# A strided attention kernel whose store of groups 20 and 21 is issued in three parts

## The chip, the cores and the metric

The kernel runs on one core of a Trainium2 chip. The metric is device time in microseconds (us): 127.87 us is the median of three runs (127.7 to 128.3). A core has a matrix engine (PE, TensorE), a vector engine (DVE), a scalar engine (ACT), a general engine (POOL, GpSimd), and SyncE (SP), which here only issues transfers. Sixteen transfer engines move data between the chip's large memory (DRAM) and the on-chip memory of 128 partitions. An instruction that issues a transfer only hands it over; the transfer then waits in a queue and adds to a semaphore when it has landed.

## The reference

```
for i in range(seq):                       # seq = 1024
    attend_positions = np.arange(0, seq, stride)          # stride = 64: 16 positions
    q = Q[:, :, i:i+1, :]; k = K[:, :, attend_positions, :]; v = V[:, :, attend_positions, :]
    scores  = np.einsum('bhqd,bhkd->bhqk', q, k) / np.sqrt(dim)
    weights = np.exp(scores - np.max(scores, axis=-1, keepdims=True))
    weights = weights / (np.sum(weights, axis=-1, keepdims=True) + 1e-10)
    result[:, :, i, :] = np.einsum('bhqk,bhkd->bhqd', weights, v)[:, :, 0, :]
```

Q, K, V and the result are 8 x 12 x 1024 x 64 in float32. Each of the 96 heads reads all its 1024 query rows, but only 16 key and 16 value rows. So Q (25.2 MB) is read once, the result (25.2 MB) is written once, and the keys and values count for little.

## The kernel before

The 96 heads are worked on in 24 groups of four heads (1 MB of Q and 1 MB of result each). `big` is an on-chip ring of 16 group buffers, 8 KB per partition each. A group's Q is loaded into its buffer (`load`), cast to bf16 half by ACT and half by POOL (`cast_a`, `cast_p`), turned by DVE (`turn`), multiplied with the keys on PE (`scores`), brought back by DVE (`spread`), and made into weights by DVE, POOL and ACT (`maximum`, `subtract`, `raise_`, `add_up`, `invert`, `normalise`). PE multiplies the weights with the values (`outputs`), and ACT copies the products over the group's Q in the same buffer (`evict`, two halves `a` and `b`). From there the group is stored.

All transfers are issued by SP, on one queue, in an order written out by hand (`order`, worked off by `issue`): all early loads; then for groups 0 to 9 a store of one group, followed for groups 2 to 9 by the load that reuses an older buffer; then stores of two groups at a time, 10 to 21; and at the very end, behind a barrier of all engines, the store of 22 and 23 (`end = send(NG - 2, 2)`). The store of 20 and 21 is thus the last but one. `send` (line 250) makes one transfer of 128 rows: a row is one partition of `big`, for two groups 16 KB in one piece on chip and four pieces of 4 KB in DRAM.

A list of operations (`Program.op`) records for each what it reads, writes and on which semaphore ("lane") it counts. Lanes whose name begins with `out` are stores; POOL waits for all of them (lines 620 to 623), clears the semaphores, and this goes on while the last store is under way, which it does not wait for. SP itself waits for the last store (line 655), and then the kernel ends. A tile `edge` (128 x 32) is declared and not used.

Of the kernel before, what the change touches and what calls it, by code (L numbers as in the profile page):

```python
# [18 lines left out]
def _ap_with(ap: bass.AP, new_ap, extra_offset: int = 0) -> bass.AP:  # L19
    return dataclasses.replace(  # L20
        ap, ap=[list(p) for p in new_ap], offset=ap.offset + extra_offset
    )


def _copy(nc, out: bass.AP, in_: bass.AP):

    sides = [
        mybir.BassSymbolicTensorAccessPattern(
            ap=side.ap, dtype=side.dtype, bass_ap=side,
            is_dma=True, for_custom_bir_dma=True,  # L30
        )
        for side in (in_, out)
    ]
    return nc.sync.add_instruction(  # L34
        mybir.InstDMACopy(
            name=nc.get_next_instruction_name(), engine=mybir.EngineType.SP,
            ins=sides[:1], outs=sides[1:], queue="qSPDynamicHW",
            mode="Copy",
        )
    )  # L40


class Program:
# [13 lines left out]
    def op(self, engine, fn, reads=(), writes=(), after=(), lane=None, gate=None, gates=(), looped=False, late=False, last=False):  # L57
        i = len(self.ops)
        deps, own = set(after), set()
        for k in reads:  # L60
            deps.add(self.writer.get(k))
            own.add(self.writer.get(k))
        for k in writes:
            deps.update(self.readers.get(k, ()))
            deps.add(self.writer.get(k))
            own.add(self.writer.get(k))
        deps.discard(None)
        for k in reads:
            self.readers.setdefault(k, []).append(i)
        for k in writes:  # L70
            self.writer[k], self.readers[k] = i, []
        self.ops.append(dict(
            engine=engine, fn=fn, lane=lane or engine, deps=deps, own=own,
            gate=gate, gates=gates, last=last, late=late, looped=looped or engine == "PE",
        ))
        return i
# [96 lines left out]
def kernel(  # L173
# [8 lines left out]
    nc = tc.nc  # L182

    B, H, S, D = Q.shape
# [3 lines left out]
    P = 128  # L188
    HG = 4
# [3 lines left out]
    SD = S * D  # L193
    NB = 16
    TURN = 2
    FIRST, LAST, ROUNDS = 2, 22, 4
    AHEAD = 3
    EPS = 1e-10
    assert NH == NG * HG == 96 and S == 1024 and D == 64 and NK == 16

# [3 lines left out]
    edge = sb.tile([P, 32], FP32, name="edge")  # L204
# [4 lines left out]
    big = sb.tile([P, NB, 32 * D], FP32, name="big")  # L209
# [25 lines left out]
    op = prog.op  # L235
# [7 lines left out]

    def store(g, n):
        b = g % NB
        op("SP", lambda: send(g, n), lane=f"out{b}",
           reads=[f"b{i % NB}{h}" for i in range(g, g + n) for h in "ab"])

    def send(g, n):
        o = big[:, g % NB : g % NB + n]  # L250
        return _copy(
            nc,
            _ap_with(out, [[16 * D, P], [2 * SD, 2 * n], [1, 16 * D]], g * HG * SD),
            _ap_with(o, [o.ap[0], [1, 1], [1, 32 * n * D]]),
        )

# [14 lines left out]
    def constants():  # L271
# [11 lines left out]
        for i in range(2):  # L283
            op("DVE", lambda i=i: nc.vector.memset(ex[i], EPS), writes=[f"ex{i}"])
        op("DVE", lambda: nc.vector.memset(k_cur, 0.0), writes=["k_cur0", "k_cur1"])
# [22 lines left out]
    def value_sums(n):  # L308
        for c in range(2):
            r = nc.tensor.matmul(  # L310
                o_ps[n][:, c, 0 : NC * D // 2],
                lhsT=perm_v[:, n].rearrange("p b e u k -> p (b e u k)"),
                rhs=v_bf[:, 6 * c : 6 * c + 6], start=True, stop=True,
            )
        return r
# [46 lines left out]
    def place_k(g):  # L362
        n = 1 if g < 2 else 2
        gap = k_cur[:, 0, 0, 32:].bitcast(I32)
        op("POOL", lambda: nc.gpsimd.tensor_copy(  # L365
            out=_ap_with(gap, [gap.ap[0], [80, 2 * n], [32, 2], [1, 16]], 160 * (g % 2)),
            in_=k_all[:, g : g + n].rearrange("p g f b x -> p (g f) b x").bitcast(I32),
        ), reads=["k_zero"] + [f"k{i % 2}{s}" for i in range(g, g + n) for s in range(4)],
           writes=[f"k_cur{i % 2}" for i in range(g, g + n)], gate=None if g == 1 else "stK")
# [9 lines left out]
    def scores(g):  # L379
        op("PE", None, reads=[f"qt{g % 2}", f"k_cur{g % 2}"], writes=[f"sc{g % 2}"],  # L380
           gates=[("turned", g + 1)] + [("stK", g // 2 + 1)] * (g % 2 == 0), gate="sc")
# [93 lines left out]
    def issue(done, flush=False):  # L475
        while order:
            kind, g, some = order[0]
            need = g + some - 1 if kind == "S" else g - NB + 1
            if not flush and need > done:
                return  # L480
            order.pop(0)
            if kind == "L":
                load(g)
            else:
                store(g, some)

    def on(f, g, *a, **how):
        if 0 <= g < NG:
            f(g, *a, **how)

    def next_keys(g):
        if g < NG:
            place_k(g)
        elif g < NG + AHEAD:
            op("POOL", lambda: nc.gpsimd.nop(), gate="stK")

    for n in range(NG + 4):
# [16 lines left out]
        if n == NG - 1:  # L514
            for g in range(AHEAD):
                op("DVE", lambda: nc.vector.nop(), gate="turned", late=True)
# [11 lines left out]
        on(normalise, n - 1)  # L528
        if n + 1 < NG + AHEAD:
            scores(n + 1)  # L530
# [14 lines left out]
    def pe_stream(sems, gates):  # L545
        pe = nc.tensor

        def score_products(g):
            for e in range(2):
                for f in range(2):  # L550
                    r = pe.matmul(  # L551
                        sc_ps[g % 2], lhsT=k_cur[:, g % 2, f, 32 * (1 - e) : 32 * (1 - e) + P],
                        rhs=_ap_with(
                            qt[g % 2], [qt[g % 2].ap[0], [D, 8], [16 * D, 2], [2, 32]],
                            extra_offset=8 * D * e + f,
                        ),
                        start=e + f == 0, stop=e + f == 2,
                    )
            r.then_inc(gates["sc"], 1)
# [14 lines left out]
        for n in range(2):  # L574
            value_sums(n).then_inc(sems["PE"], 1)
        for g in range(AHEAD):
            pe.wait_ge(gates["turned"], g + 1)
# [3 lines left out]
        with pe.Fori(0, NG // TURN):  # L581
            for j in range(TURN):
                pe.wait_ge(gates["turned"], j + AHEAD + 1)
                if j:
                    pe.wait_ge(gates["stK"], (j + AHEAD) // 2 + 1)
                score_products(j + AHEAD)
# [33 lines left out]
    with tc.tile_critical(sync_engine=mybir.EngineType.Pool, no_gpsimd_drain=True) as landed:  # L620
        for sem, n in pending:
            nc.gpsimd.wait_ge(sem, n)
        nc.clear_and_free_semaphores(sems)
    tc.no_sync_barrier()
    end = send(NG - 2, 2)
    tc.declare_no_dep(end.ins, landed, reason="waits for the older stores alone")
# [33 lines left out]
```

## Time and profile before

| | |
|---|---|
| median of three runs | 127.87 us (127.7 to 128.3) |
| profiled execution | 127.99 us |
| its span in the trace | 126.2 us |
| busy: DVE, ACT, POOL, PE | 75%, 72%, 67%, 47% of the span |
| moved by the transfer engines | 51.15 MB, mean 405 GB/s |
| stores of two groups | 7, of 2048 KB each, median 16.9 us from issue to landing |

Times in the trace count from the start of the span; the profiled execution is 1.8 us longer than its span. Views used below: the page with its busy shares and its 40 slices; the waits of SP's queue; the chain of work that ended last, in order of time; the timelines of SP and POOL; groups of instructions by source line; and a table of busy time by stage, whose last two columns are the mean busy share of the sixteen transfer engines and the GB/s that they moved. Transfers issued on SP's queue are marked SPq. A transfer packet counts in the stage in which it starts.

### The profile page before, as it was taken

The numbers are of one execution on the slowest core, as the hardware profiler recorded it, in microseconds if no ns is written. First come the engines' busy times: TensorE is split into PE (matmuls) and PEld (weight loads), VectorE is DVE, ScalarE is ACT, GpSimd is POOL, SyncE is SP. The second block draws the span as 40 slices with busy tenths as digits, with TensorE's granted clock in tenths as the row PEclk, the third lists the DMA queues.
The fourth block names the chain that finished last, engine by engine and source line by source line (L and its number), as shares of the span: only waits on it lengthen the run. The fifth ranks groups of instructions, "written<-read, shape, count | busy, mean of one in ns | idle before, by whom it ended". The sixth has DMA issues, their size and how long they took to land.

```text
span 126.2 us, 1652 instructions
## 1 busy us (share of the span) xinstructions
PE 59.9 (47%) x496; PEld 29.0 (23%) x496; DVE 94.9 (75%) x160; ACT 90.6 (72%) x106; POOL 84.2 (67%) x108
## 2 busy tenths in 40 slices
PE   0002822539766456645666456645666369700000
PEld 0001100114333223333333223333333135300000
DVE  5349699399999999999999999999998985000000
ACT  4043977635999899998999899998997597910000
POOL 3018550929899899999999899998999586000000
PEclk9999995555899999999999999999999999996555
DMA  3999989999899989989999989989999999999990
GB/s 65 355 398 428 467 363 478 405 447 467 363 478 405 447 361 426 493 356 428 465 392 436 470 374 462 462 358 493 389 421 426 428 415 431 431 431 421 426 415 31
DMA packets 6803, 51.15 MB, mean 405 GB/s; under 512 B 3760, under 2 KB 3760, under 8 KB 3760
## 3 DMA queue, kind: packets, MB, share of 16 engines
q1 hardware_dynamic: 6800, 51.12, 97.3%
q14 instruction: 3, 0.02, 0.0%
HBM read 25.95 MB, written 25.17 MB: 405 GB/s over the span
## 4 chain that ended last, share of the span: by engine, by line
DVE 61%; PE 9%; DMA 6%; issue 3%; ACT 2%; POOL 2%; SPq 1%; ACTq 1%; DVEq 1%
DVE qt L356 21%; DVE s_t L384 11%; DVE top L391 11%; DVE total L409 10%; PE sc L551 7%; DMA big<-in_V_dram 6%; DVE w_t L431 5%; DVE rec L416 3%; PE o L565 2%; POOL s_t L398 1%; DVE v_all L334 1%; ACT big L447 1%; SPq L34 1%; ACT qb L347 1%; ACTq L161 1%
## 5 line engine op out<-in xcount | busy, mean ns | idle before, releaser
L447 ACT COPY big<-o 128x1024 f32<-128x1024 f32 x48 | 46.2, 1014 | 1.6 <-PE o L565 1.6
L551 PE MATMUL sc<-qt,k_cur 128*128 128x512 bf16 x108 | 32.3, 424 | 27.4 <-DVE qt L356 22.1
L398 POOL TENSOR_TENSOR s_t<-s_t,top 128x512 f32<-128x512 f32 x24 | 25.4, 1059 | 10.2 <-DVE top L391 10.2
L565 PE MATMUL o<-v_cur,w_t 64*64 64x256 bf16 x384 | 26.5, 277 | 10.3 <-DVE w_t L431 7.7
L356 DVE STREAM_TRANSPOSE qt<-qb 128x1024 int32<-128x1024 int32 x24 | 28.9, 1203 | 0.0
L423 POOL TENSOR_TENSOR w_n<-ex,rec 128x512 bf16<-128x512 f32 x24 | 25.5, 1063 | 2.8 <-DVE rec L416 1.1
L352 POOL CAST qb<-big 128x1024 bf16<-128x1024 f32 x24 | 25.1, 1045 | 0.7 <-DMA big<-in_Q_dram 0.7
L347 ACT CAST qb<-big 128x1024 bf16<-128x1024 f32 x24 | 25.3, 1055 | 0.3 <-DMA big<-in_Q_dram 0.3
L565 PEld LDWEIGHTS o<-v_cur,w_t 64*64 64x64 bf16 x384 | 19.9, 108 | 22.8 <-ACT big L447 16.1
L404 ACT ACTIVATE ex<-s_t 128x512 f32<-128x512 f32 x24 | 15.2, 632 | 9.5 <-POOL s_t L398 9.0
L384 DVE STREAM_TRANSPOSE s_t<-sc 128x512 f32<-128x512 f32 x24 | 16.3, 678 | 3.9 <-PE sc L551 2.6
L551 PEld LDWEIGHTS sc<-qt,k_cur 128*128 128x128 bf16 x108 | 8.7, 101 | 45.1 <-DVE qt L356 30.2
L409 DVE TENSOR_REDUCE total<-ex 128x32 f32<-128x544 f32 x24 | 17.0, 707 | 0.6 <-ACT ex L404 0.6
L391 DVE TENSOR_REDUCE top<-s_t 128x32 f32<-128x512 f32 x24 | 15.5, 648 | 0.1
L431 DVE STREAM_TRANSPOSE w_t<-w_n 128x256 int32<-128x256 int32 x24 | 10.4, 435 | 1.2 <-POOL w_n L423 1.2
L416 DVE RECIPROCAL rec<-total 128x32 f32<-128x32 f32 x24 | 7.5, 312 | 0.0
L310 PE MATMUL o<-big,perm_v 128*128 128x384 bf16 x4 | 1.5, 521 | 12.0 <-POOL big L318 12.0
L373 POOL COPY v_cur<-v_all 128x256 int32<-128x256 int32 (+1 forms) x13 | 5.0, 386 | 0.5 <-PE o L565 0.5
L365 POOL COPY k_cur<-k_all 128x128 int32<-128x128 int32 (+1 forms) x13 | 3.7, 283 | 2.1 <-ACT k_all L303 1.8
L293 ACT CAST big<-big 128x384 bf16<-128x384 f32 x1 | 0.5, 511 | 5.1 <-DMA big<-in_K_dram 5.1
L294 POOL CAST big<-big 128x384 bf16<-128x384 f32 x1 | 0.5, 509 | 5.0 <-DMA big<-in_K_dram 5.0
L303 DVE COPY k_all<-big 32x384 bf16<-32x384 bf16 x6 | 3.5, 591 | 0.1
(19 smaller groups left out, 16.2 us busy)
## 6 DMA issues: line engine op xcount, KB each, us to landing
big<-in_Q_dram SPq DMA_DIRECT2D x24, 1024.0 KB, 12.3
out_dram<-big SPq DMA_DIRECT2D x7, 2048.0 KB, 16.9
out_dram<-big SPq DMA_DIRECT2D x10, 1024.0 KB, 14.2
big<-in_K_dram SPq DMA_DIRECT2D x1, 384.0 KB, 5.8
big<-in_V_dram SPq DMA_DIRECT2D x1, 384.0 KB, 8.2
```

Source lines behind the costliest of these rows:

```text
L347: op("ACT", lambda: nc.scalar.copy(b[:, half:], q[:, half:]), reads=[f"b{g % NB}{h}" for h in "ab"], writes=[f"qb{g % 4}1"])
L352: op("POOL", lambda: nc.gpsimd.tensor_copy(out=b[:, 0:half], in_=q[:, 0:half]), reads=[f"b{g % NB}{h}" for h in "ab"] + [f"qb{g % 4}1"] * ...
L356: return nc.vector.transpose(qt[g % 2].bitcast(I32), qb[g % 4].bitcast(I32))
L384: return nc.vector.transpose(s_t[g % 2].rearrange("p n k -> p (n k)"), sc_ps[g % 2])
L391: return nc.vector.tensor_reduce(out=top[g % 2], in_=s_t[g % 2], op=ALU.max, axis=mybir.AxisListType.X)
L398: op("POOL", lambda: nc.gpsimd.tensor_tensor(out=s_t[g % 2], in0=s_t[g % 2], in1=top[g % 2].unsqueeze(2).to_broadcast([P, 32, NK]), op=ALU ...
L409: return nc.vector.tensor_reduce(out=total[g % 2], in_=ex[g % 2], op=ALU.add, axis=mybir.AxisListType.X)
L423: op("POOL", lambda: nc.gpsimd.tensor_tensor(out=_ap_with(w_n[g % 2], [w_n[g % 2].ap[0], [64, 8], [1, 2], [32, 2], [2, NK]]), in0=ex[g % 2 ...
L431: return nc.vector.transpose(w_t[g % 2].rearrange("p t m -> p (t m)").bitcast(I32), w_n[g % 2].rearrange("p n k -> p (n k)").bitcast(I32),)
L447: op("ACT", lambda: nc.scalar.copy(to, o), reads=[f"o{h}"], writes=[f"b{g % NB}{'ab'[h]}"], gate=None if g == NG - 1 or (g, h) == (NG - 3, ...
L551: r = pe.matmul(sc_ps[g % 2], lhsT=k_cur[:, g % 2, f, 32 * (1 - e) : 32 * (1 - e) + P], rhs=_ap_with(qt[g % 2], [qt[g % 2].ap[0], [D, 8], ...
L565: r = pe.matmul(o_ps[h][rows, t // 2, 256 * (t % 2) : 256 * (t % 2) + 256], lhsT=w_t[g % 2][rows, 4 * h + t], rhs=v_cur[rows, g % 2].rearr ...
```

## The change

The store of groups 20 and 21 becomes three transfers with the same 128 rows in all: rows 0 to 111 on SP's queue; rows 126 and 127 on SP's queue, as a transfer of their own; and rows 112 to 125 on POOL's queue. In front of the last, POOL issues a load of four rows of 64 bytes from Q into the tile `edge`, which nothing reads. Each of the new transfers has its own semaphore, and its name begins with `out`, so POOL also waits for these before it clears the semaphores. All other stores, the last one too, stay at 128 rows.

```diff
+    SPLIT = 20
...
     def store(g, n):
         b = g % NB
-        op("SP", lambda: send(g, n), lane=f"out{b}",
-           reads=[f"b{i % NB}{h}" for i in range(g, g + n) for h in "ab"])
-
-    def send(g, n):
-        o = big[:, g % NB : g % NB + n]
+        rows = [f"b{i % NB}{h}" for i in range(g, g + n) for h in "ab"]
+        if g != SPLIT:
+            op("SP", lambda: send(g, n), lane=f"out{b}", reads=rows)
+            return
+        op("SP", lambda: send(g, n, 0, 112), lane=f"out{b}", reads=rows)
+        op("SP", lambda: send(g, n, 126, 2), lane="out_two", reads=rows)
+        op("POOL", lambda: nc.gpsimd.dma_start(
+            edge[0:4, 0:16], _ap_with(Q, [[D, 4], [1, 16]]),
+        ), lane="out_edge", writes=["edge"])
+        op("POOL", lambda: nc.gpsimd.dma_start(*parts(g, n, 112, 14)), lane="out_some", reads=rows)
+
+    def parts(g, n, p, rows):
+        o = big[p : p + rows, g % NB : g % NB + n]
+        return (
+            _ap_with(out, [[16 * D, rows], [2 * SD, 2 * n], [1, 16 * D]], g * HG * SD + 16 * D * p),
+            _ap_with(o, [o.ap[0], [16 * D, 2 * n], [1, 16 * D]]),
+        )
+
+    def send(g, n, p=0, rows=P):
+        o = big[p : p + rows, g % NB : g % NB + n]
         return _copy(
             nc,
-            _ap_with(out, [[16 * D, P], [2 * SD, 2 * n], [1, 16 * D]], g * HG * SD),
+            _ap_with(out, [[16 * D, rows], [2 * SD, 2 * n], [1, 16 * D]], g * HG * SD + 16 * D * p),
             _ap_with(o, [o.ap[0], [1, 1], [1, 32 * n * D]]),
         )
```

On SP, from the last load to the end of the recorded program, before (-) and with the change (+); `at_ACT` is the count of ACT's finished copies, and x5 means five such rows in a row:

```order
 L34 DMA out_dram<-big 128x2x1024 [waits at_ACT]
 L34 DMA big<-in_Q_dram 128x2048 [waits at_out7]
-L34 DMA out_dram<-big 128x4x1024 [waits at_ACT] x6
-L263 UNCONDITIONAL_BRANCH [waits at_ACT]
+L34 DMA out_dram<-big 128x4x1024 [waits at_ACT] x5
+L34 DMA out_dram<-big 112x4x1024 [waits at_ACT]
+L34 DMA out_dram<-big 2x4x1024
+L279 UNCONDITIONAL_BRANCH [waits at_ACT]
```

The sixth two-group store has become two transfers that stand in its place; the last store (not in the piece) still comes behind the barrier.

On POOL, from the last normalisations to the barrier, with the change (`w_n` are the normalised weights; before, the same rows stand there without the two rows that begin with DMA):

```order
L439 TENSOR_TENSOR w_n_77<-ex_75,rec_85 128x8x2x32 [waits at_DVE]
L389 COPY v_cur<-v_all 128x256 [waits at_PE]
L439 TENSOR_TENSOR w_n_78<-ex_76,rec_86 128x8x2x32 [waits at_DVE]
L253 DMA edge<-in_Q_dram 4x16
L256 DMA out_dram<-big 14x4x1024 [waits at_ACT]
L279 UNCONDITIONAL_BRANCH
L161 UNCONDITIONAL_BRANCH
L161 NO_OP [waits SP_49]
```

The two issues stand behind POOL's last arithmetic and ahead of the barrier; the second waits for ACT's copy of group 21, as SP's store does.

## The prediction

> **What bounds the kernel now.** I read the page first: the busy shares, the 40 slices, and the queues.
>
> ```profile
> PE 59.9 (47%) x496; PEld 29.0 (23%) x496; DVE 94.9 (75%) x160; ACT 90.6 (72%) x106; POOL 84.2 (67%) x108
> ...
> DMA  3999989999899989989999989989999999999990
> GB/s 65 355 398 428 467 363 478 405 447 467 363 478 405 447 361 426 493 356 428 465 392 436 470 374 462 462 358 493 389 421 426 428 415 431 431 431 421 426 415 31
> ...
> q1 hardware_dynamic: 6800, 51.12, 97.3%
> q14 instruction: 3, 0.02, 0.0%
> ...
> DVE 61%; PE 9%; DMA 6%; issue 3%; ACT 2%; POOL 2%; SPq 1%; ACTq 1%; DVEq 1%
> ```
>
> No compute engine is above 75%, but the transfer engines are busy in nearly every slice, and all of it is on one queue, SP's (q1). The chain on the page (last line) names DVE for 61% and the transfers for 6%, but it leads back from the last computation, so I looked at what the end itself waits for: the waits of SP's queue, the last pieces of the chain in order of time, and SP's and GpSimd's timelines near the end.
>
> ```profile
> SPq L655 <- DMA out_dram<-big: 13.7, 1, 13.7
> ...
> 109.01 1.01 ACT big L447
> 110.02 0.91 ACTq L161
> ...
> 106.71 4.93 SPq L34 DMA_DIRECT2D out_dram<-big  x2
> ...
> 105.58 1.06 POOL L423 TENSOR_TENSOR w_n<-ex,rec 128x512 bf16<-128x512 f32 x1
> ```
>
> The last eviction is over at about 110.9 us. SP issues the store of groups 20 and 21 at 106.71 and that of 22 and 23 at about 111.1 (the two together take until 106.71 + 4.93 = 111.64, and one issue takes 0.54). Then SP waits 13.7 us for the last store alone. So the last 14 us of the kernel are transfers already in the queue. GpSimd has nothing after 105.58 + 1.06 = 106.64. A table by stage of those 14 us is the view on which all the rest stands (columns: busy times of the engines with counts, then TensorE's clock, the share of the 16 transfer engines, GB/s):
>
> ```profile
> 118.00:122.90 4.90, 0.00 (x0) 0.00 (x0) 0.00 (x0) 0.00 (x0) 0.00 (x0) 0.50 1.01 428
> 122.90:123.60 0.70, 0.00 (x0) 0.00 (x0) 0.00 (x0) 0.00 (x0) 0.00 (x0) 0.50 0.28 117
> 123.60:124.25 0.65, 0.00 (x0) 0.00 (x0) 0.00 (x0) 0.00 (x0) 0.00 (x0) 0.50 0.06 25
> 124.25:124.90 0.65, 0.00 (x0) 0.00 (x0) 0.00 (x0) 0.00 (x0) 0.00 (x0) 0.50 0.06 25
> 124.90:126.20 1.30, 0.00 (x0) 0.00 (x0) 0.00 (x0) 0.00 (x0) 0.00 (x0) 0.50 0.00 0
> ```
>
> At 428 GB/s each of 16 engines moves 26.75 GB/s, so one row of a two-group store (16,384 bytes) takes 0.61 us on its engine. The view counts a row where it starts: 117 GB/s x 0.70 us is 82 KB, five rows; 25 GB/s x 0.65 us is 16 KB, one row, and again one row in the next window. A share of 0.06 is one engine of 16. So the engines do not finish together: most are through by about 123.6, some four run on to about 124.2, and one single engine is still moving rows until about 125. A 128-row store gives each engine eight rows (128/16). **The end is set by one engine that is about one row behind the next and two to three behind most.** The trace names no engine, so which of the sixteen it is stays unknown.
>
> **The change part by part.** (a) The store of 20 and 21 on SP shrinks from 128 to 112 rows, 112/16 = seven per engine: 0.61 us less on every engine's queue. (b) Two rows go on SP's queue as a store of their own: +0.61 us on two engines. (c) Fourteen rows go on GpSimd's queue: +0.61 us on fourteen engines, if each takes one. The sum over the engines is 112 + 2 + 14 = 128 rows, as before; no byte is saved. If (b) and (c) fell on sixteen different engines, nothing would change; if they overlap on two, two engines have nine rows and two have seven. The time of the end is that of the late engine, so it goes by its own count: seven rows, -0.61; eight, 0; nine, +0.61. These are the bounds of this term. Two of sixteen engines could be the ones with seven, so I take eight, 0.
>
> (d) When they run matters less than how many there are. GpSimd's rows are issued from about 107 on, beside SP's queue, which then still holds nearly three stores (20 and 21, issued at 106.7, land 4.9 us before the last, at about 120.5: 13.8 us of work). A row served early pushes the engine's own rows back by 0.61, and the seven-row share gives that back. The end of an engine that has eight rows in all stays.
>
> (e) Issues on SP: one more, the 2-row one. The 23 loads and 17 stores issued so far cost (ns, least, median, most), and the third line has the stores' time from issue to landing:
>
> ```profile
> L34 SPq DMA_DIRECT2D big<-in_Q_dram x23: 471/594/3505, 1.9 to 77.9; - x23
> L34 SPq DMA_DIRECT2D out_dram<-big x17: 538/615/750, 33.3 to 111.1; - x17
> ...
> DMA to landing us min/median/max: 9.3/14.3/21.2
> ```
>
> One issue is 0.54 to 0.75 us. It lies between 107.3 and 108.0, and SP waits there anyway for the eviction that ends at 110.9: nothing.
>
> (f) Issues on GpSimd: two, a kind the trace of before does not show on that engine. Nearest rows: 0.59 us (the median above) to 3.5 us (the longest issue on SP), so 1.2 to 7.0 us for both; none cheaper than 0. I take 1.2, the common case of the nearest row. From 106.64 they end at 107.8, or at 113.6. Behind them on GpSimd stand only the barrier that SP's last store passes, the wait for the older stores, and the clearing of semaphores. The last store is now issued at 111.1 and so could be up to 2.5 us late. It has cover: its 2 MB take 4.9 us at 428 GB/s and have landed at about 111.1 + 14.3 = 125.4, so the first engines start on it only at about 118. Cost 0 up to some 11 us of issue time; beyond that each microsecond counts in full. GpSimd's later waits on three more stores lie before SP's own wait: the older stores have landed about 4.9 us before the last. 0.
>
> (g) The load of four short rows and the extra completions: at most a few small packets on an engine. Bounds: 0 to one row time, 0.61, since even a full row would not cost more; I take 0.02. (h) GpSimd's rows may move in four pieces of 4 KB each. The slowest full slice above ran at 355 GB/s, the last stage at 428: a row would take 0.74, so 0 to +0.13; I take 0, because stages with 8 KB rows (the one-group stores) run in the same slices, of 355 to 493 GB/s.
>
> Sum against the profiled time, 127.99 us (span 126.2 and 1.8 around it): 0 + 0 + 0.02 = 128.0. The median of the three runs is 127.87, 0.12 below the profiled one; the forecast on that scale is **127.9 us**.
>
> In the program's order the sixth two-group store on SP has become two stores and nothing else moved there; on GpSimd the two new issues stand behind the last normalisation (group 23), so they delay no computation.
>
> **Rivals.** *The late engine gets seven rows.* Then it ends 0.61 us earlier, at about 124.4 instead of 125.0; the engines that run to about 124.2 don't decide even so, and one of them with nine rows would end at about 124.8, so the gain is 0.2 to 0.6 us: 127.3 to 127.7. For it: there is exactly one such engine, and a change of one row is of the size of its lag. Against it: by the rows, only two places in sixteen.
>
> [...]
>
> *Two engines at one part of the memory (slower).* In a 128-row store each engine has its own eight rows, and 428 GB/s show that sixteen run side by side. Seven rows per engine cannot be that same division. If engines then draw on the same partitions at once, the two share one rate and a row takes 1.23 instead of 0.61. Place: the 112-row store, at about 113 to 118. Price: +0.61 for each row that meets another; two such rows per engine give +1.2, 129.1, all seven +4.3, 132.2. It decides as soon as one engine loses more than its lead on the late one, or the late one meets another once. For it: no store in the trace has another number of rows than 128, so another division was never shown harmless. Against it: the rate sags nowhere in the stage of stores, and rows that meet may spread out again.
>
> [...]
>
> *GpSimd's queue costs on the path (slower).* Issue times of over 11 us in all, or nine rows on the late engine: 128.5 to 129. For it: the operation is new there. Against it: the cover in (f), and only two engines can have nine rows.
>
> *The change doesn't do what it says:* the 14 rows land on few engines. With seven rows each on two engines, these end 6 x 0.61 = 3.7 us later, about 130 to 131. I count it with the slower cases.
>
> **How the numbers follow.** Late engine keeps eight rows: 0.42. Seven rows: 0.30 (0.12 from two places in sixteen, the rest a chance of its own for the rule on engines 14 and 15). Shared partitions: 0.15. GpSimd's costs and rows on few engines: 0.13. A measurement of this kernel can tell about 0.5% (0.64 us) from no change, so one row, 0.48%, is just short of it. Of the 0.30 I put 0.15 on faster by over 0.5%, since the late engine's lag and the runs (127.7 to 128.3) scatter by as much as is missing, and 0.15 within; 0.03 of the first case goes to faster for what I don't see. Faster: 0.18. Within 0.5%: 0.39 of the first case, 0.15, and 0.06 of the costs: 0.60. Slower: 0.15 and 0.07, that is 0.22. The range for 8 in 10: down to the full row and a little more, 127.1, up to two rows that meet, 129.0. The likeliest case alone: 127.6 to 128.1.
>
> **What would show it.** In the changed profile: SP's timeline with two issues in a row at 106.7; a new queue under the queues with 14 rows; GpSimd with two issues ending before 111; the windows after 122.9 with the same 25 GB/s twice (eight rows), once (seven) or three times (nine). Shared partitions would show as a rate below 420 GB/s between 113 and 123. Wrong would be: an end more than one row earlier; a last store that starts late because of GpSimd; a tail of several engines.

## The result, and the profile after

The changed kernel takes 129.74 us (median of fourteen executions, 128.5 to 131.99), against 127.88 us before (127.7 to 128.3): slower by 1 to 1.5%, and the fastest execution with the change lies above the slowest before. The ratio is 1.0095 (95% interval 1.0073 to 1.0118) over the nine executions within 1.5% of the fastest, which is the least that the change costs; the medians of all stand 1.0145 to 1. The forecast was 127.9, with a range up to 129.0.

The profiled execution took 130.9 us, one of the longer ones, with a span of 129.1. From its page: the slices (the last four are those to look at), the queues, and the issues of the three parts.

```profile
span 129.1 us, 1657 instructions
...
DMA  2999999999999899999999998999999999999940
GB/s 74 338 394 422 447 437 416 447 437 416 437 437 426 371 424 421 431 449 393 437 452 386 447 464 371 462 454 393 426 431 416 424 431 426 416 415 362 401 188 25
...
q1 hardware_dynamic: 6788, 50.89, 95.2%
q0 software_dynamic: 112, 0.23, 0.5%
...
out_dram<-big SPq DMA_DIRECT2D x1, 1792.0 KB, 15.7
...
out_dram<-big POOLq DMA_DIRECT2D x1, 224.0 KB, 9.2
out_dram<-big SPq DMA_DIRECT2D x1, 32.0 KB
```

The 14 rows did go through another queue, q0. The transfer engines are as busy as before to the 38th slice, but in the 37th and 38th they move less: 362 and 401 GB/s, against 421 and 426 before. In these slices single rows take up to 1.57 us, against 0.616 for the usual one (packet list, below). The 39th, 188 at four tenths, is a tail. The waits of SP's queue and the timeline of GpSimd show when the last issues came:

```profile
SPq L671 <- DMA out_dram<-big: 15.6, 1, 15.6
...
106.79 1.06 POOL L439 TENSOR_TENSOR w_n<-ex,rec 128x512 bf16<-128x512 f32 x1 [0.19 <-DVE rec L432]
107.79 0.74 POOL L253 DMA_DIRECT2D edge<-in_Q_dram  x1
108.52 0.61 POOL L256 DMA_DIRECT2D out_dram<-big  x1
```

GpSimd's two issues are over at 109.1, before the barrier; SP then waits 15.6 us for the last store instead of 13.7. The last normalisation starts 1.2 us later than before (106.79 against 105.58), and the last store is issued about 1 us later. That costs nothing: the engines still have older stores to move, and in the run with the whole store on SP (below) the normalisation starts nearly as late, at 106.53, and that execution takes 127.92 us. The same six stages of both kernels (last columns: share of the transfer engines, GB/s), first before:

```profile
108.00:113.00 5.00, 1.51 (x18) 0.71 (x16) 0.00 (x0) 2.75 (x3) 0.00 (x0) 1.00 1.01 429
113.00:117.00 4.00, 0.00 (x0) 0.00 (x0) 0.00 (x0) 0.00 (x0) 0.00 (x0) 0.66 0.99 422
117.00:121.00 4.00, 0.00 (x0) 0.00 (x0) 0.00 (x0) 0.00 (x0) 0.00 (x0) 0.50 1.01 430
121.00:123.00 2.00, 0.00 (x0) 0.00 (x0) 0.00 (x0) 0.00 (x0) 0.00 (x0) 0.50 0.98 418
123.00:124.00 1.00, 0.00 (x0) 0.00 (x0) 0.00 (x0) 0.00 (x0) 0.00 (x0) 0.50 0.20 82
```

and with the change:

```profile
108.00:113.00 5.00, 2.48 (x28) 1.13 (x23) 0.33 (x1) 3.73 (x4) 1.13 (x2) 1.00 1.00 423
113.00:117.00 4.00, 0.00 (x0) 0.00 (x0) 0.00 (x0) 0.00 (x0) 0.00 (x0) 0.65 1.04 414
117.00:121.00 4.00, 0.00 (x0) 0.00 (x0) 0.00 (x0) 0.00 (x0) 0.00 (x0) 0.50 1.02 377
121.00:123.00 2.00, 0.00 (x0) 0.00 (x0) 0.00 (x0) 0.00 (x0) 0.00 (x0) 0.50 0.91 369
123.00:124.00 1.00, 0.00 (x0) 0.00 (x0) 0.00 (x0) 0.00 (x0) 0.00 (x0) 0.50 0.66 279
124.00:130.00 6.00, 0.00 (x0) 0.00 (x0) 0.00 (x0) 0.00 (x0) 0.00 (x0) 0.50 0.12 49
```

Up to 113 the two agree. GpSimd's rows run from 113 to 117, at 414 GB/s against 422. From 117 to 121, while the 112 rows run, the rate is 377 instead of 430 at a full share, and the engines no longer end together: before, 82 GB/s are left for 123 to 124 and 3 after it; now engines are at work until about 128.

The trace's list of packets shows on which engine the time is lost. It names no engine, but on a full queue a 16 KB row takes 0.616 us and the next on the same engine starts 0.613 us after it, so an engine's packets can be followed backwards from its last. Before, the last engine ends at 124.98, and none of its last 24 rows took over 0.63 us. With the change the last engine ends at 127.91. It has seven of the 112 rows, one of GpSimd's 14 (in four pieces) and the eight of the last store, and six of the seven took 1.23, 1.15, 0.74, 0.80, 1.27 and 1.49 us. That is 2.98 us over the usual time. Without it this engine would have ended at 124.93, as good as before: in this execution the slow rows of the 112-row store are the whole loss.

### The profile page after: what moved, and what is told of

It is laid out like the page before. It is cut to its first block, busy times and chain, and to the rows that moved or that the text cites. A ratio compares the mean times of both kernels' runs of the same rounds, so it can differ in the third digit from the quotient of the medians.

```text
span 129.1 us, 1657 instructions
## 1 busy us (share of the span) xinstructions
PE 61.1 (47%) x496; PEld 29.7 (23%) x496; DVE 95.1 (74%) x160; ACT 90.5 (70%) x106; POOL 85.5 (66%) x110
## 4 chain that ended last, share of the span: by engine, by line
DVE 60%; PE 10%; DMA 6%; issue 3%; ACT 2%; POOL 2%; SPq 2%; ACTq 1%; DVEq 1%
DVE qt L372 20%; DVE s_t L400 11%; DVE top L407 10%; DVE total L425 10%; PE sc L567 7%; DMA big<-in_V_dram 6%; DVE w_t L447 4%; DVE rec L432 3%; PE o L581 2%; DVE v_all L350 1%; SPq L34 1%; POOL s_t L414 1%; ACT big L463 1%; ACT qb L363 1%; ACTq L161 1%
## 5 line engine op out<-in xcount | busy, mean ns | idle before, releaser
L581 PE MATMUL o<-v_cur,w_t 64*64 64x256 bf16 x384 | 27.4, 283 | 10.3 <-DVE w_t L447 8.2
L581 PEld LDWEIGHTS o<-v_cur,w_t 64*64 64x64 bf16 x384 | 20.5, 111 | 23.1 <-ACT big L463 16.9
L407 DVE TENSOR_REDUCE top<-s_t 128x32 f32<-128x512 f32 x24 | 15.6, 648 | 0.1
L350 DVE TENSOR_SCALAR v_all<-big,s_sel 128x768 bf16<-128x768 bf16 x4 | 2.9, 756 | 1.2 <-ACT qb L363 1.2
```

The source lines that it names most:

```text
L407: return nc.vector.tensor_reduce(out=top[g % 2], in_=s_t[g % 2], op=ALU.max, axis=mybir.AxisListType.X)
L581: r = pe.matmul(o_ps[h][rows, t // 2, 256 * (t % 2) : 256 * (t % 2) + 256], lhsT=w_t[g % 2][rows, 4 * h + t], rhs=v_cur[rows, g % 2].rearr ...
```

## The experiments

Below, a measured time is the median, with the lowest and the highest execution; the ratio is to the kernel before, run beside it, with its 95% interval. Three theories were on the table. **Shared partitions:** 112 rows are divided over the engines in a way that lets several draw on the same part of the on-chip memory at once. **GpSimd's queue:** the new queue costs. **Row counts:** an engine has nine rows, or GpSimd's shares fall elsewhere in each execution.

### 112 and 16 rows, both on SP

```diff
         op("SP", lambda: send(g, n, 0, 112), lane=f"out{b}", reads=rows)
-        op("SP", lambda: send(g, n, 126, 2), lane="out_two", reads=rows)
-        op("POOL", ...edge...); op("POOL", ...14 rows...)
+        op("SP", lambda: send(g, n, 112, 16), lane="out_two", reads=rows)
```

> The store of 20 and 21 goes as 112 rows and 16 rows, both on SP's queue; GpSimd issues nothing. Every engine has 7 + 1 = 8 rows. Shared partitions (a division into seven rows per engine lets engines draw on the same partitions): slower, 129 to 132 us, with GB/s below 400 between about 115 and 122 as in the changed kernel. GpSimd's queue as the cause: 127.9, no slower stage. Row counts as the cause (an engine with nine rows): 127.9, since all have eight.

Measured: 130.55 us (130.51 to 131.87), ratio 1.0234 (1.0203 to 1.0266). The same stage as above, 117 to 121:

```profile
117.00:121.00 4.00, 0.00 (x0) 0.00 (x0) 0.00 (x0) 0.00 (x0) 0.00 (x0) 0.50 0.97 336
```

The loss is there without GpSimd and with eight rows for every engine. It is larger than the change's, so neither other theory is needed for it.

### The whole store on SP, and the short load alone on GpSimd

```diff
-        op("SP", lambda: send(g, n, 0, 112), ...); op("SP", lambda: send(g, n, 126, 2), ...)
+        op("SP", lambda: send(g, n), lane=f"out{b}", reads=rows)
         op("POOL", lambda: nc.gpsimd.dma_start(edge[0:4, 0:16], ...), lane="out_edge", writes=["edge"])
-        op("POOL", ...14 rows...)
```

> The store of 20 and 21 goes whole, 128 rows on SP as before; of the change only the load of four short rows on GpSimd's queue is left. Shared partitions: no change, 127.9. GpSimd's queue as the cause: part of the loss stays, 128.2 to 130, and the executions scatter as those of the changed kernel do. Row counts: no change.

Measured: 127.95 us (127.8 to 128.08), ratio 1.0006 (0.9997 to 1.0014). The new queue with its short load costs nothing that can be measured, and brings no scatter.

### Two stores of 64 rows

```diff
+        op("SP", lambda: send(g, n, 0, 64), lane=f"out{b}", reads=rows)
+        op("SP", lambda: send(g, n, 64, 64), lane="out_two", reads=rows)
```

(in place of the change's four issues)

> The store of 20 and 21 goes as two stores of 64 rows on SP, four rows per engine each, eight in all. Shared partitions: if a store of half the partitions keeps only half of the memory's ways busy, each row takes about 1.23 us instead of 0.61, eight rows +4.9 us: about 132.8, with about 215 GB/s while these rows run. Row counts and GpSimd's queue: 127.9.

Measured: 131.52 us (130.64 to 131.88), ratio 1.0275 (1.024 to 1.0309), so +3.6 us of the 4.9 that eight halved rows would cost. The stage shows why the theory is taken seriously:

```profile
117.00:121.00 4.00, 0.00 (x0) 0.00 (x0) 0.00 (x0) 0.00 (x0) 0.00 (x0) 0.50 1.00 242
```

242 GB/s at a full share is 56% of the 430 before. By the packet list 59 rows start in this stage instead of 105, and 36 of the 59 took over 1.0 us, where the usual row takes 0.62.

### Group 21 through GpSimd's queue, 128 rows

```diff
+        op("SP", lambda: send(g, 1), lane=f"out{b}", reads=rows)
+        op("POOL", lambda: nc.gpsimd.dma_start(*parts(g + 1, 1, 0, P)), lane="out_some", reads=rows)
```

> Group 20 is stored on SP with 128 rows of 8 KB, group 21 on GpSimd's queue, also with 128 rows of 8 KB, in place of one store of both. Shared partitions: the division of 128 rows is kept, so no change, 127.9 (127.5 to 128.3). GpSimd's queue as the cause: 1 MB instead of 0.23 MB goes through it, so slower than the changed kernel or as slow, 129 and up. Row counts: eight half rows twice on every engine, no change.

Measured: 128.03 us (127.89 to 128.28), ratio 1.0008 (0.9997 to 1.0019). From its page:

```profile
q0 software_dynamic: 272, 1.05, 2.0%
```

The stage from 117 to 121 runs at 440 GB/s. More than four times the change's bytes go through GpSimd's queue at no cost, as long as the rows are 128.

### Partitions 32 to 95, twice

Same two stores of 64 rows, same places in DRAM; only the partitions that are read differ.

```diff
-    def send(g, n, p=0, rows=P):
-        o = big[p : p + rows, g % NB : g % NB + n]
+    def send(g, n, p=0, rows=P, at=None):
+        at = p if at is None else at
+        o = big[at : at + rows, g % NB : g % NB + n]
...
+        op("SP", lambda: send(g, n, 0, 64, 32), lane=f"out{b}", reads=rows)
+        op("SP", lambda: send(g, n, 64, 64, 32), lane="out_two", reads=rows)
```

> Two stores of 64 rows on SP as in the run with 64 and 64 rows, to the same places of DRAM, but both read partitions 32 to 95 (so the two groups' result holds these rows twice, and the other rows of these groups are not stored). Only what is read on chip differs. [...] If the cause is how 64-row stores fall on DRAM, or their number of rows per engine: 131.5 as there, about 240 GB/s at 117 to 121.

Measured: 127.99 us (127.89 to 128.33), ratio 1.0000 (0.9988 to 1.0013).

```profile
117.00:121.00 4.00, 0.00 (x0) 0.00 (x0) 0.00 (x0) 0.00 (x0) 0.00 (x0) 0.50 1.03 438
```

This settles it for stores of 64 rows: 438 GB/s instead of 242, with the rows per store, the rows per engine, the number of issues and the addresses in DRAM unchanged. What decides between these two runs is which partitions their stores read. For the 112 rows the same cause is argued, not shown: they have the same mark, single rows that take up to twice their time and more (1.57 us with the change, against 0.616), and the other causes tried are excluded; but no trace says which partitions an engine reads there, and no run changed these alone.

### The change with two short rows in place of four

```diff
-            edge[0:4, 0:16], _ap_with(Q, [[D, 4], [1, 16]]),
+            edge[0:2, 0:16], _ap_with(Q, [[D, 2], [1, 16]]),
```

> The change with a load of two short rows in place of four, so GpSimd's two transfers have 2 + 14 = 16 shares instead of 18. If the place where GpSimd's shares fall moves on from one execution to the next by the shares issued (16 brings it back, 18 does not), the executions agree within 0.5%, at some value between 128.5 and 132, where those of the change scatter from 128.5 to 132.0. If the scatter comes from how rows meet, it stays: some 2.5% between executions. Shared partitions in either case: slower than before.

Measured: 130.9 us (129.48 to 133.07), ratio 1.0185 (1.0144 to 1.0226). The scatter stays, 2.8% between the executions. If 16 shares bring the place back, as was supposed (no trace names the engine a share falls on), shares that move on from one execution to the next are not its cause, or not alone.

### 112, 2 and 14 rows, all on SP

```diff
-        op("POOL", ...edge...); op("POOL", ...14 rows...)
+        op("SP", lambda: send(g, n, 112, 14), lane="out_some", reads=rows)
```

> The change with its 14 rows on SP's queue instead of GpSimd's, no short load: 112, 2 and 14 rows, all on SP. Shared partitions: slower as with 112 and 16 rows, 129.5 to 132, and little scatter. If GpSimd's queue were needed for the loss: 127.9.

Measured: 130.47 us (129.47 to 130.97), ratio 1.0168 (1.013 to 1.0205), 336 GB/s at 117 to 121. Slower without GpSimd, as expected; but the scatter of 1.2% is there too, against the "little" that was expected.

### 112 and 16 rows for groups 10 and 11

```diff
-    SPLIT = 20
+    SPLIT = 10
```

(in the kernel with 112 and 16 rows on SP)

> 112 and 16 rows on SP, but for the store of groups 10 and 11, nine to ten stores' time earlier, instead of 20 and 21. Shared partitions with full queues from there on: what is lost is not given back, 129 to 131 us, and the slow stage lies near 80 to 90. If engines have spare time before the last stores that takes it up: 127.9 to 128.3.

Measured: 129.08 us (128.62 to 129.21), ratio 1.0073 (1.0049 to 1.0097): 1.2 us lost where the same split at 20 loses 2.7. The stage of 90 to 94 runs at 406 GB/s, against 430 before. The loss lies at the low end of the first expectation. Its slow rows start between 91 and 94, not near 80 to 90: the store stands only five two-group stores earlier, 5 x 4.9 = 24.5 us. So part of the loss does not reach the end when six whole stores still follow; which wait or stage takes it up was not tried.

### One part alone

First the 112 rows alone, then the small parts alone.

```diff
         op("SP", lambda: send(g, n, 0, 112), lane=f"out{b}", reads=rows)
-        (the 2 rows, the short load and the 14 rows)
```

> Of the store of 20 and 21 only the 112 rows on SP are left; the other 16 rows are not stored (0.26 MB less). If the 112 rows meet at the partitions: every engine has one row less (127.9 - 0.61 = 127.3), and the loss of 1.5 to 2.7 us comes on top: 128.8 to 130, with 330 to 380 GB/s at 117 to 121. If the small parts (2 rows, 14 rows, GpSimd) cause the loss: 127.3, over 410 GB/s.

Measured: 129.87 us (129.14 to 130.66), ratio 1.017 (1.0111 to 1.023), with less to store. The rate at 117 to 121 is below the 430 before, but above the 330 to 380 that was expected:

```profile
117.00:121.00 4.00, 0.00 (x0) 0.00 (x0) 0.00 (x0) 0.00 (x0) 0.00 (x0) 0.50 1.00 393
```

```diff
-        op("SP", lambda: send(g, n, 0, 112), lane=f"out{b}", reads=rows)
         (the 2 rows, the short load and the 14 rows)
```

> Of the store of 20 and 21 only the small parts are left: 2 rows on SP, the short load and 14 rows on GpSimd's queue; rows 0 to 111 are not stored (1.8 MB less). Seven rows less on every engine: 127.9 - 7 x 0.61 = 123.6 if the small parts are harmless, at most one row more (124.2) where two rows fall on one engine or meet once. If they cause the loss of 1.5 to 2.7 us: 125.1 to 126.3.

Measured: 123.70 us (123.69 to 123.73), ratio 0.967 (0.9654 to 0.9686). From the waits of SP's queue in the two, first 112 alone, then the small parts:

```profile
SPq L666 <- DMA out_dram<-big: 14.4, 1, 14.4
```

```profile
SPq L670 <- DMA out_dram<-big: 8.6, 1, 8.6
```

The 112 rows are enough for the whole loss: one row less per engine should give 127.3, and they take 129.87, 2.6 us more. The small parts end within 0.1 us of the 123.6 that the row time gives, and four executions agree within 0.04 us. So scatter, too, comes with the 112 rows alone (1.2%), and not with GpSimd's queue, its 14 rows or its short load alone. Why it is wider where both stand together (2.7% with the change, 2.8% with two short rows) is not known.

## Why the prediction was wrong

**The bound was read rightly.** The end is the queue of transfers; GpSimd's and SP's issues are hidden, and the last store is what SP waits for.

**Step (a) failed.** It said "112/16 = seven per engine: 0.61 us less on every engine's queue", a count of rows at one price. The price 0.61 had been read from stores of 128 rows alone. The 112 rows by themselves cost 2.6 us more than the count gives. What the count left out is that rows of the new division can take longer: in the profiled execution six of the seven on the last engine took 2.98 us too long between them. This one term carries the sign of the result. The eight rows taken for the engine that ends last were right (seven and one of GpSimd's) and decided nothing.

**(d) to (h) held.** GpSimd's issues took 0.74 and 0.61 us, 1.35 together where 1.2 was taken. The short load and the new queue gave 1.0006, 1 MB through the queue 1.0008, and the small parts by themselves 123.70 where the count gives 123.6. In (h), a row in four pieces of 4 KB takes 4 x 0.159 = 0.64 us by the packet list (median of the 56 pieces), against 0.62 whole.

**The rival of shared partitions came nearest**, with its sign (a rate below 420 GB/s between 113 and 123: 414, 377 and 369) and nearly its place: it named 113 to 118, and the slow rows start at 115 to 122. (Each row is a partition of its own, so within one store no two engines read the same partition, as the rival put it; what they share, if that is the cause, no run shows.) Its price was too small: 129.1 for two rows that meet, where the median is 129.74 and the last engine of the profiled execution has six slow rows. Its chance, 0.15, was too low, and the range stopped at that price. Of the two reasons against it, that the rate sags nowhere weighed nothing, since no store of before had another division, as the line before it said; and that rows that meet may spread out again did not come true, since six slow ones came one behind the other on the engine that ends last. The tail of several engines, which the forecast named as a sign of being wrong, came too (ends at 125.8, 127.2 and 127.9). A cost that a trace cannot show should have widened the range upwards.

**The rival of seven rows** did not come about. In the run with the small parts alone, the packets of the engine that ends last have one of GpSimd's rows, and the four times of 123.70 fit seven rows less (123.6), not eight (123.0). Whether one row less on that engine would help in a whole kernel stays open. Of the 0.30 given to this rival, 0.18 was for a rule on engines 14 and 15: no run shows such a rule, and no trace numbers the engines; what the profile of the change shows is seven of the 112 rows and one of GpSimd's on the engine that ends last, and none of its executions took less than 128.5 us. The forecast's own case (eight rows, no change) is what the runs with 128 rows show.

## What to carry to other kernels

Where transfers set the end, try first to divide a store by columns and to keep all partitions in each piece: here 128 rows in two halves of the columns, one on SP's and one on GpSimd's queue, cost nothing (ratio 1.0008), while 112 and 16 rows or 64 and 64 rows cost 2.7 and 3.6 us. If rows must be split, look at which partitions stand in one piece; with 64 rows in each store it made the whole difference here: 0 to 63 and then 64 to 127 ran at 242 GB/s, 32 to 95 twice at 438. (The latter does not store all rows; no run has a split of this kind that does.) And a price read from one shape is no price for another (0.61 us a row from stores of 128 rows missed 2.6 us with 112); when the trace has no row of the new shape, its bound belongs in the range.

## What the runs showed of the hardware that was not expected

Executions of one program whose last store but one is split after row 112 or row 64 scatter by about 1% or more (129.14 to 130.66 with 112 rows alone, 128.5 to 131.99 with the change), where kernels with 128-row stores, and the one that reads partitions 32 to 95 twice, stay within about 0.6%. The trace's list of packets shows where the time goes: of the 16 KB rows, these took over 1.0 us, where the usual one takes 0.62:

```
kernel                        16 KB rows   over 1.0 us   longest, us
before                           896            1           1.03
the change                       882           16           1.57
112 and 16 rows on SP            896           13           2.72
64 and 64 rows                   896           53           2.37
partitions 32 to 95, twice       896            1           1.04
```

A few slow rows are enough: sixteen of 882 in the change, one of which has its like in the kernel before. They count because they gather: four of the rows over 1.0 us are on the engine that ends last, and three on the one before it. The longest with 112 and 16 rows (2.72, 2.67 and 2.29 us) are rows of the 16-row store. What delays these rows, and why the executions of one program differ, no run shows.
